# A trunk layer on one core: the fifth and sixth weight loads put behind splits on VectorE, and the last output bank finished in two halves

## The chip, the core and the metric

The kernel runs on one core of a Trainium2 chip. The core has TensorE for matrix products (PE; its weight loads are listed apart as PEld), VectorE (DVE), ScalarE (ACT), GpSimd (POOL) and SyncE (SP), which here issues nearly all transfers between HBM and on-chip memory; sixteen DMA engines carry them. Each engine works through its own list of instructions in order and waits on semaphores that the others raise. The metric is device microseconds of one execution.

## The reference

One decoder layer on 256 tokens of width 2048, in fp32: three groups of self-attention heads, cross-attention to a memory of 256 tokens, a gated feed-forward part with a short convolution, and a last RMS norm.

```python
h = rms_norm(x, g_mix)
qa, ka, va, qb, kb, vb, qc, kc, vc = split(h @ w_in)
x = x + concat(diff_attn(qa, ka, va), moba(qb, kb, vb), dilated(qc, kc, vc)) @ w_out
x = x + memory_cross_attention(rms_norm(x, g_cross), rms_norm(mem, g_mem), ...)
x = x + (silu(causal_dwconv3(h @ w_gate)) * (h @ w_up)) @ w_down     # h = rms_norm(x, g_ffn)
out = rms_norm(x, g_final)
```

## The kernel before

Every weight is streamed once from HBM. It is cut into **pieces** of 128 x 2048 fp32 (1 MB), numbered in the order in which they are used; piece 0 is the first, so the fifth and sixth are pieces 4 and 5. A piece lands in one of four buffers called `raw`. Before use it is split in two halves, h = 0 and 1: ACT copies half of `raw` to a rounded high part `hi` (L142), then DVE takes the difference as `lo` (L149). A product is then made of high times high, high times low and low times high. Half h of piece p has the number 2p + h, and **step i** of the main loop (L1023) multiplies half i: step 0 is the first half of piece 0, step 8 the first half of piece 4.

What is issued at a step, and so the order on each engine, is written out by hand: at step i the loop first asks for loads (L1027, L1028), then issues the split of half i + 4 (high parts on ACT, then what `before(i, ...)` registered, then low parts on DVE), then the products of half i, then what `after(i, ...)` registered.

At the start it is otherwise, since the inputs themselves come in: x (2 MB) and pieces 0, 1 and 2 are loaded in parts, taking turns (L933 to L946). For halves 2 to 7 the split is registered by `after(i, ...)` (L982), together with `put_x`, which scales two blocks of x into `hT` (L194 on ACT, L197 on DVE). Only from step 4 on does the main loop issue splits. So the split of half 8 (piece 4), which stands at the head of step 4, is on ACT's list **ahead** of the splits of halves 6 and 7 (piece 3), which stand behind the products of steps 4 and 5. On ACT this gives: half 5, half 8, x blocks, half 6, half 9, x blocks, half 7, a square of x, half 10 (piece 5), a square of x, half 11, and then four copies L354, with which the first chunk of output columns leaves PSUM.

The first chunk is done after step 7. It fills four PSUM banks; five are set aside for such chunks. Step 8 begins the second chunk: its first column block takes the free fifth bank, its second waits for the first bank of the old chunk, which is free after ACT's L354 and DVE's L355.

A fourth `raw` buffer is allocated at L950 as `hold`, and a copy of it at step 8 (L952) keeps it from the loads until then. So piece 3 goes into the buffer of piece 0, piece 4 into that of piece 1, piece 5 into that of piece 2, each when DVE has taken the last low part out of it.

At the end, `down` (L868) multiplies by w_down. All eight output banks (2 token tiles t, 4 column blocks n of 512) gather over 44 pieces; the products of the last two pieces are made bank by bank, and each bank is added to x as soon as it is whole (L890), squared (L891) and multiplied by the gain (L898). With all sums of a token tile in hand, three small DVE operations (L899 to L901) and a power on POOL (L903) give the factor r, and `finish` (L858) scales the four blocks and stores them.

Of the kernel before, what the change touches and what calls it, by code (L numbers as in the profile page):

```python
# [11 lines left out]
F32 = mybir.dt.float32  # L12
F32R = mybir.dt.float32r
AF = mybir.ActivationFunctionType
ALU = mybir.AluOpType
AX = mybir.AxisListType

P = 128
D = 2048
# [6 lines left out]
KF = DFF // P  # L26
# [8 lines left out]
HALF = 1024  # L35
NRAW = 4
# [26 lines left out]
def trunk(ctx, tc, x, mem, w_in, w_out, diff_lambda, rel_bias_table, w_cq, w_ckv, w_co, w_up, conv, w_down,  # L63
# [25 lines left out]
    def any_tile():  # L89

        turn[0] += 1
        return (acc_tile if turn[0] % 8 < NACC else at_tile)()

    def small(n, name, bufs=4):
        return tmp.tile([P, n], F32, tag=f"sm_{name}", name=name, bufs=bufs)
# [10 lines left out]
    pieces = []  # L106
# [6 lines left out]
    def new_raw(p):  # L113
        if p.raw is None:
            p.raw = wpool.tile([P, 2 * HALF], F32, tag="raw", name="raw", bufs=NRAW)

    def load(p):
        new_raw(p)
        at = 0
        for src in p.srcs:  # L120
            n = 1
            for _, c in src.ap[1:]:
                n *= c
            dst = p.raw[:, at:at + n]
            if len(src.ap) == 3:
                dst = dst.rearrange("p (k n) -> p k n", k=src.ap[1][1])
            SP.dma_start(dst, src)
            at += n
        assert at == 2 * HALF
# [28 lines left out]
    def before(i, f):  # L158
        pre.setdefault(i, []).append(f)

    def after(i, f):
        post.setdefault(i, []).append(f)
# [100 lines left out]
    def square_sum(src, acc, n=512):  # L263
        junk = tmp.tile([P, 512], mybir.dt.bfloat16, tag="junk", name="junk", bufs=1)
        ACT.activation(junk[:, :n], src, AF.Square, accum_out=acc)
# [557 lines left out]
    def xtok(t, c):  # L823

        return xT[:, 4 * c + 2 * t:4 * c + 2 * t + 2, :].rearrange("p k n -> p (k n)")
# [5 lines left out]
    outs = {}  # L831
# [11 lines left out]
        hi, lo = parts[k]  # L843
        DVE.tensor_tensor(lo, ffn["a"][:, k, :], hi.bitcast(F32), op=ALU.subtract)

    def down_mm(p, k, h, t, n):
        hi, lo = p.parts[h]
        ah, al = (a[:, t * P:(t + 1) * P] for a in parts[k])
        o = outs[t, 2 * h + n]
        wh, wl = hi[:, n * 512:(n + 1) * 512], lo[:, n * 512:(n + 1) * 512]  # L850
        PE.matmul(o, ah, wh, start=(k == 0), stop=False)  # L851
        PE.matmul(o, ah, wl, start=False, stop=False)  # L852
        PE.matmul(o, al, wh, start=False, stop=(k == KF - 1))  # L853

    ss3 = small(8, "ss3", 1)
    fin = {}

    def finish(n, t, og, r):  # L858
        col = slice(n * 512, (n + 1) * 512)
        if t and n % 2:  # L860
            DVE.scalar_tensor_tensor(og[:, col], xtok(t, n), r, gfin["t"][:, col], op0=ALU.mult, op1=ALU.mult)
        elif t or n < 2:
            ACT.activation(og[:, col], og[:, col], AF.Copy, scale=r)
        else:
            (DVE, POOL)[n - 2].tensor_scalar_mul(og[:, col], og[:, col], r)
        SP.dma_start(out[t * P:(t + 1) * P, col], og[:, col])

    def down(k):  # L868
        def f(p, h):
            if k == 0 and h == 0:  # L870
                for t in range(NT):
                    for n in range(4):
                        outs[t, n] = any_tile()
            fin[k] = p
            if k < KF - TAIL:
                for t in range(NT):
                    for n in range(2):
                        down_mm(p, k, h, t, n)
            elif k == KF - 1 and h == 1:
                done = None  # L880
                for t in range(NT):
                    og = wpool.tile([P, 2 * HALF], F32, tag="raw", name="raw", bufs=NRAW)
                    ms = small(2, "msf")
                    ss = ss3[:, 4 * t:4 * t + 4]
                    for n in range(4):
                        for kk in range(KF - TAIL, KF):
                            down_mm(fin[kk], kk, n // 2, t, n % 2)
                        col = slice(n * 512, (n + 1) * 512)
                        xc = xtok(t, n)
                        DVE.tensor_tensor(xc, outs[t, n], xc, op=ALU.add)  # L890
                        square_sum(xc, ss[:, n:n + 1])  # L891
                        if done:
                            for m in ((3, 0, 1), (2,), (), ())[n]:
                                finish(m, *done)
                        gains = ((), (0,), (), (2,)) if t else ((0,), (1,), (2,), (3,))
                        for m in gains[n]:
                            col = slice(m * 512, (m + 1) * 512)
                            DVE.tensor_tensor(og[:, col], xtok(t, m), gfin["t"][:, col], op=ALU.mult)  # L898
                    DVE.reduce_sum(ms[:, 0:1], ss[:, :3], axis=AX.X)  # L899
                    DVE.tensor_scalar(ms[:, 0:1], ms[:, 0:1], 1.0 / D, EPS, op0=ALU.mult, op1=ALU.add)  # L900
                    DVE.scalar_tensor_tensor(ms[:, 1:2], ss[:, 3:4], 1.0 / D, ms[:, 0:1], op0=ALU.mult, op1=ALU.add)  # L901
                    r = small(1, "rfin")
                    POOL.tensor_tensor(r, ms[:, 1:2], mhalf, op=ALU.pow)  # L903
                    done = t, og, r
                for n in range(4):
                    finish(n, *done)
        return f
# [38 lines left out]
    load_x(12, 4)  # L946

    hold = wpool.tile([P, 2 * HALF], F32, tag="raw", name="raw", bufs=NRAW)  # L950
    POOL.memset(hold[:, :1], 0.0)
    before(8, lambda: DVE.tensor_copy(small(1, "held", 1), hold[:, :1]))  # L952


    warm = acc_tile()
    for _ in range(24):
        PE.transpose(warm[:, :P], ident, ident)
# [3 lines left out]
    def put_x(k):  # L961
        for f in (high, low):
            for j in range(2):
                f(xblock(k + j), MIX, lambda: hT["h"], k + j)

    def split(i):
        split_hi(pieces[i // 2], i % 2)
        split_lo(pieces[i // 2], i % 2)
# [8 lines left out]
    put_x(2)  # L977
    split(1)
    load(pieces[3])
    nload = 4  # L980
    for i in range(6):
        after(i, lambda i=i: (put_x(2 * i + 4), split(i + 2)))  # L982
    for c in range(4):
        square_part(c + 5, "x", c, lambda c=c: xpart(c))
    norm_factors(10, "x")
# [37 lines left out]
    for i in range(2 * len(pieces)):  # L1023
        cur[0] = i
        new = []
        while nsplit < min(2 * len(pieces), i + 1 + LEAD if i > 2 else 0):
            while nload < len(pieces) and nload <= nsplit // 2 + NRAW - 2:  # L1027
                load(pieces[nload])  # L1028
                nload += 1
            new.append((pieces[nsplit // 2], nsplit % 2))  # L1030
            nsplit += 1
        for p, h in new:
            split_hi(p, h)
        for f in pre.pop(i, []):
            f()
        for p, h in new:
            split_lo(p, h)
        pieces[i // 2].mm(pieces[i // 2], i % 2)
        for f in post.pop(i, []):
            f()  # L1040
# [32 lines left out]
```

## Time and profile before

| what | value |
|---|---|
| time, median of three runs | 1251.67 us (1251.46 to 1252.79) |
| the profiled execution | 1252.27 us, of which the span is 1250.5 us |
| PE busy | 1235.8 us |
| DVE, ACT busy | 830.8 us, 630.0 us |
| the rest outside the span | 1.77 us |

A row of the timeline gives the start, the duration, the engine, the line, the operation and its tiles, and in brackets how long the engine sat idle before it and what ended that. "SPq" is SP issuing a transfer; the time until that transfer has landed stands in the row on DMA issues. TensorE's clock is given as the share of full speed that was granted: 1.00 is 2.4 GHz, 0.50 is 1.2 GHz.

### The profile page before, as it was taken

How to read it: one execution, taken by the hardware profiler on the slowest of the kernel's cores; microseconds unless marked ns; L12 is line 12 of the kernel's file. 1: busy time of each engine (PE TensorE's matmuls, PEld its weight loads, DVE VectorE, ACT ScalarE, POOL GpSimd, SP SyncE). 2: the span in 40 equal slices, each digit the busy share in tenths (PEclk: the TensorE clock that was granted, in tenths of full speed). 3: DMA queues.
4: the chain of work that ended last, by engine and by line, in shares of the span. 5: the costliest groups of instructions: out<-in, count | busy, mean ns of one | idle time of the engine just before them, and what ended most of it. 6: DMA issues, size and time to landing. Idle time of an engine off the chain costs nothing.

```text
span 1250.5 us, 17611 instructions
## 1 busy us (share of the span) xinstructions
PE 1235.8 (99%) x6928; PEld 1072.4 (86%) x6928; DVE 830.8 (66%) x1351; ACT 630.0 (50%) x979; POOL 12.3 (1%) x23
## 2 busy tenths in 40 slices
PE   8999999999999999999999999999999999999997
PEld 7888888988888899888888888888888888888885
DVE  5755676576568877876767768667776854445445
ACT  6544555556455656545445444444444544444444
POOL 0000000000000000000000000000000000000000
PEclk9999999999999999999999999999999999999998
DMA  7855554555566555565556565565556555555541
GB/s 275 273 172 191 189 170 159 182 184 156 177 227 217 170 169 164 204 206 169 170 201 196 175 202 190 183 201 184 187 180 202 192 193 180 200 176 194 187 150 68
DMA packets 104835, 233.26 MB, mean 187 GB/s; under 512 B 4208, under 2 KB 14768, under 8 KB 98992
## 3 DMA queue, kind: packets, MB, share of 16 engines
q1 hardware_dynamic: 104576, 231.85, 55.3%
q8 instruction: 54, 0.88, 0.3%
q10 hardware_dynamic: 144, 0.26, 0.1%
q14 instruction: 29, 0.24, 0.1%
q0 software_dynamic: 32, 0.02, 0.0%
HBM read 230.00 MB, written 2.12 MB: 186 GB/s over the span
## 4 chain that ended last, share of the span: by engine, by line
issue 58%; PE 37%; DMA 2%; DVE 2%; ACT 0%; POOL 0%; DVEq 0%; POOLq 0%; SPq 0%; ACTq 0%
PE acc L295 16%; PE acc L302 8%; PE acc L341 3%; PE acc L343 3%; PE acc L342 3%; DMA raw<-in_w_in 1%; PE at L401 1%; DMA xin<-in_x 1%; DVE lo L149 1%; PE at L420 0%; PE at L444 0%; DVE hT L197 0%; PE acc L298 0%; PE acc L297 0%; PE at L472 0%
## 5 line engine op out<-in xcount | busy, mean ns | idle before, releaser
L149 DVE TENSOR_TENSOR lo<-raw,hi 128x1024 fp32r<-128x1024 f32 x423 | 517.1, 1223 | 360.0 <-ACT hi L142 359.5
L142 ACT CAST hi<-raw 128x1024 fp32r<-128x1024 f32 x423 | 442.8, 1048 | 473.1 <-PE acc L295 272.4
L295 PE MATMUL acc<-hT,hi 128*128 128x512 f32 x1776 | 625.4, 395 | 3.5 <-ACT hi L142 3.3
L302 PE MATMUL acc<-hT,lo 128*128 128x256 f32 x1840 | 512.0, 280 | 0.6 <-DVE lo L149 0.6
L295 PEld LDWEIGHTS acc<-hT,hi 128*128 128x128 f32 x1776 | 334.4, 188 | 78.1 <-ACT hi L142 3.7
L302 PEld LDWEIGHTS acc<-hT,lo 128*128 128x128 f32 x1840 | 345.3, 188 | 1.4 <-DVE lo L149 1.2
L295 PE MATMUL at<-hT,hi 128*128 128x512 f32 x528 | 187.5, 392 | 0.0
L302 PE MATMUL at<-hT,lo 128*128 128x256 f32 x528 | 147.6, 280 | 0.0
L295 PEld LDWEIGHTS at<-hT,hi 128*128 128x128 f32 x528 | 99.1, 188 | 21.8
L302 PEld LDWEIGHTS at<-hT,lo 128*128 128x128 f32 x528 | 99.2, 188 | 0.0
L851 PE MATMUL acc<-hi,ah 128*128 128x512 f32 x220 | 87.8, 399 | 0.0
L853 PE MATMUL acc<-hi,al 128*128 128x512 f32 x220 | 86.7, 394 | 0.0
L852 PE MATMUL acc<-lo,ah 128*128 128x512 f32 x220 | 86.2, 392 | 0.0
L341 PE MATMUL acc<-hi,hT 128*128 128x256 f32 (+1 forms) x224 | 75.0, 335 | 0.0
L343 PE MATMUL acc<-hi,hT 128*128 128x256 f32 (+1 forms) x224 | 73.9, 330 | 0.0
L342 PE MATMUL acc<-lo,hT 128*128 128x256 f32 (+1 forms) x224 | 73.8, 330 | 0.0
L851 PE MATMUL at<-hi,ah 128*128 128x512 f32 x132 | 52.7, 399 | 0.0
L853 PE MATMUL at<-hi,al 128*128 128x512 f32 x132 | 52.0, 394 | 0.0
L788 ACT ACTIVATE y<-y 128x256 f32<-128x256 f32 x44 | 18.4, 419 | 66.3 <-DVE y L784 66.3
L852 PE MATMUL at<-lo,ah 128*128 128x512 f32 x132 | 51.7, 392 | 0.0
L853 PEld LDWEIGHTS acc<-hi,al 128*128 128x128 f32 x220 | 41.3, 188 | 10.8
L852 PEld LDWEIGHTS acc<-lo,ah 128*128 128x128 f32 x220 | 41.3, 188 | 9.8
(159 smaller groups left out, 1003.2 us busy)
## 6 DMA issues: line engine op xcount, KB each, us to landing
raw<-in_w_up SPq DMA_DIRECT2D x88, 1024.0 KB, 5.0
raw<-in_w_in SPq DMA_DIRECT2D x45, 1024.0 KB, 5.2
raw<-in_w_down SPq DMA_DIRECT2D x44, 1024.0 KB, 4.9
raw<-in_w_out SPq DMA_DIRECT2D x12, 1024.0 KB, 5.3
raw<-in_w_ckv SPq DMA_DIRECT2D x8, 1024.0 KB, 5.6
raw<-in_w_out SPq DMA_DIRECT2D x8, 512.0 KB, 4.9
raw<-in_w_cq SPq DMA_DIRECT2D x4, 1024.0 KB, 5.3
raw<-in_w_co SPq DMA_DIRECT2D x4, 1024.0 KB, 5.2
```

Of the source, the lines that this page charges most:

```text
L142: ACT.copy(hi, p.raw[:, h * HALF:(h + 1) * HALF])
L149: DVE.tensor_tensor(lo, p.raw[:, h * HALF:(h + 1) * HALF], hi.bitcast(F32), op=ALU.subtract)
L295: PE.matmul(accs[n], w, x, start=(i == 0), stop=False)
L302: PE.matmul(accs[n][:, :S], lo[:, j, n * P:(n + 1) * P], src()[:, korder[i], :S], start=False, stop=(i == len(korder) - 1))
L341: PE.matmul(o, xh, hi[:, j, :], start=(i == 0), stop=False)
L342: PE.matmul(o, xh, lo[:, j, :], start=False, stop=False)
L343: PE.matmul(o, xl, hi[:, j, :], start=False, stop=(i == len(korder) - 1))
L401: PE.matmul(out, a[u], b[w], start=first and i == 0, stop=last and i == 2)
L788: after(cur[0] + 1 + n, lambda: ACT.activation(gate[k], gate[k], AF.Silu))
L851: PE.matmul(o, ah, wh, start=(k == 0), stop=False)
L852: PE.matmul(o, ah, wl, start=False, stop=False)
L853: PE.matmul(o, al, wh, start=False, stop=(k == KF - 1))
```

## The change

At the start: `hold` and its copy at step 8 are gone, so that four `raw` buffers are in use from the beginning. Piece 3 is loaded into the free fourth buffer. Pieces 4 and 5 are no longer loaded by the main loop. A new function `load_behind` writes one column of the buffer by a DVE memset and then asks for the load; it is registered behind the split of half 5 (piece 4) and behind the split of half 7 (piece 5). The main loop asks for no load before step 6.

At the end: of the last bank (t = 1, n = 3) the products of the last two pieces are made for columns 0 to 255 first and then for columns 256 to 511, the latter in a bank of their own, and are added and squared apart. For t = 1 the gain products of blocks 2 and 3 stand behind the last additions, and the last scalings are done by ACT and DVE's simple multiply. For t = 0, ACT and POOL scale two blocks each.

```diff
-    def down_mm(p, k, h, t, n):
+    def down_mm(p, k, h, t, n, c0=0, c1=512, own=None):
...
-        PE.matmul(o, ah, wh, start=(k == 0), stop=False)
+        o, first = (outs[t, 2 * h + n][:, c0:c1], 0) if own is None else (own, KF - TAIL)
+        wh, wl = (a[:, n * 512 + c0:n * 512 + c1] for a in (hi, lo))
+        PE.matmul(o, ah, wh, start=(k == first), stop=False)
...
     def finish(n, t, og, r):
         col = slice(n * 512, (n + 1) * 512)
-        if t and n % 2:
-            DVE.scalar_tensor_tensor(og[:, col], xtok(t, n), r, gfin["t"][:, col], op0=ALU.mult, op1=ALU.mult)
-        elif t or n < 2:
+        if t:
+            if n % 2:
+                ACT.activation(og[:, col], og[:, col], AF.Copy, scale=r)
+            else:
+                DVE.tensor_scalar_mul(og[:, col], og[:, col], r)
+        elif n < 2:
             ACT.activation(og[:, col], og[:, col], AF.Copy, scale=r)
         else:
-            (DVE, POOL)[n - 2].tensor_scalar_mul(og[:, col], og[:, col], r)
+            POOL.tensor_scalar_mul(og[:, col], og[:, col], r)
         SP.dma_start(out[t * P:(t + 1) * P, col], og[:, col])
+
+    def gained(og, t, n):
+        col = slice(n * 512, (n + 1) * 512)
+        DVE.tensor_tensor(og[:, col], xtok(t, n), gfin["t"][:, col], op=ALU.mult)
...
+                    parts_of = ((0, 0, 512), (1, 0, 512), (2, 0, 512)) + (((3, 0, 256), (3, 256, 512)) if t else ((3, 0, 512),))
...
-    hold = wpool.tile([P, 2 * HALF], F32, tag="raw", name="raw", bufs=NRAW)
-    POOL.memset(hold[:, :1], 0.0)
-    before(8, lambda: DVE.tensor_copy(small(1, "held", 1), hold[:, :1]))
...
     load(pieces[3])
-    nload = 4
+    nload = 6
     for i in range(6):
         after(i, lambda i=i: (put_x(2 * i + 4), split(i + 2)))
+
+    def load_behind(p):
+        new_raw(p)
+        DVE.memset(p.raw[:, :1], 0.0)
+        load(p)
+
+    after(3, lambda: load_behind(pieces[4]))
+    after(5, lambda: load_behind(pieces[5]))
...
-            while nload < len(pieces) and nload <= nsplit // 2 + NRAW - 2:
+            while i > 5 and nload < len(pieces) and nload <= nsplit // 2 + NRAW - 2:
```

On SP the loads of pieces 3 to 7 stand in a row; the names in brackets are the semaphores that each load waits for (DMAHW a transfer, DVE and Activation those engines). Before:

```order
L924 DMA xin<-in_x 128x1024 [waits DMAHW4_49]
L127 DMA raw<-in_w_in 128x4x512 [waits DMAHW5_49,DVE_49]
L127 DMA raw<-in_w_in 128x4x512 [waits DMAHW6_49,DMAHW0_49,DVE_49]
L127 DMA raw<-in_w_in 128x4x512 [waits DMAHW3_49,DMAHW7_49,DMAHW2_49,DVE_49]
L127 DMA raw<-in_w_in 128x4x512 [waits DMAHW6_49,DVE_49]
```

On SP after the change, the same five places:

```order
L940 DMA xin<-in_x 128x1024 [waits DMAHW4_49]
L127 DMA raw<-in_w_in 128x4x512 [waits DMAHW5_49]
L127 DMA raw<-in_w_in 128x4x512 [waits DMAHW6_49,DVE_49,Activation_49]
L127 DMA raw<-in_w_in 128x4x512 [waits DMAHW0_49,DMAHW7_49,DVE_49,Activation_49]
L127 DMA raw<-in_w_in 128x4x512 [waits DMAHW3_49,DMAHW2_49,Activation_49]
```

The load of piece 3 no longer waits for DVE, those of pieces 4 and 5 still do, and the load of piece 6 stands behind that of piece 5.

What DVE is to have done by then is seen on its own list. DVE before, from the low part of half 5 to the copies that free the first banks (L149 is a low part, L197 a block of x, L227 a sum of squares, L355 such a copy):

```order
L149 TENSOR_TENSOR lo<-raw,hi 128x1024 x2
L197 SCALAR_TENSOR_TENSOR hT<-xin,hT 128x256 x2
L149 TENSOR_TENSOR lo<-raw,hi 128x1024 x2
L197 SCALAR_TENSOR_TENSOR hT<-xin,hT 128x256 x2
L149 TENSOR_TENSOR lo<-raw,hi 128x1024 x2
L227 TENSOR_TENSOR sq<-sq 128x1024
L149 TENSOR_TENSOR lo<-raw,hi 128x1024
L355 TENSOR_TENSOR mg<-acc,mg 128x256 x4
```

DVE after the change, the same stretch; the low parts are those of halves 5; 8; 6 and 9; 7; 10; 11:

```order
L149 TENSOR_TENSOR lo<-raw,hi 128x1024
L998 MEMSET raw 128x1
L149 TENSOR_TENSOR lo<-raw,hi 128x1024
L197 SCALAR_TENSOR_TENSOR hT<-xin,hT 128x256 x2
L149 TENSOR_TENSOR lo<-raw,hi 128x1024 x2
L197 SCALAR_TENSOR_TENSOR hT<-xin,hT 128x256 x2
L149 TENSOR_TENSOR lo<-raw,hi 128x1024
L998 MEMSET raw 128x1
L149 TENSOR_TENSOR lo<-raw,hi 128x1024
L227 TENSOR_TENSOR sq<-sq 128x1024
L149 TENSOR_TENSOR lo<-raw,hi 128x1024
L355 TENSOR_TENSOR mg<-acc,mg 128x256 x4
```

The first memset, with the load of piece 4 behind it, stands between the low parts of halves 5 and 8; the second memset, with the load of piece 5 behind it, now stands between the low parts of halves 7 and 10.

At the end, DVE's list for the second token tile, before (L890 adds a bank to x, L898 is a gain product, L861 a last scaling):

```order
L890 TENSOR_TENSOR xin<-acc,xin 128x512
L898 TENSOR_TENSOR raw<-xin,gfin 128x512
L899 TENSOR_REDUCE msf<-ss_92 128x1
L900 TENSOR_SCALAR msf<-msf 128x1
L901 SCALAR_TENSOR_TENSOR msf<-ss_92,msf 128x1
L861 SCALAR_TENSOR_TENSOR raw<-xin,rfin,gfin 128x512 x2
```

DVE at the end, after the change (L900 and L902 add to x, L873 is a gain product, L864 a last scaling):

```order
L900 TENSOR_TENSOR xin<-acc,xin 128x512
L902 TENSOR_TENSOR xin<-acc,xin 128x256
L910 TENSOR_REDUCE msf<-ss_92 128x1
L911 TENSOR_SCALAR msf<-msf 128x1
L873 TENSOR_TENSOR raw<-xin,gfin 128x512
L914 SCALAR_TENSOR_TENSOR msf<-ss_92,msf 128x1
L915 SCALAR_TENSOR_TENSOR msf<-ss_92,msf 128x1
L873 TENSOR_TENSOR raw<-xin,gfin 128x512
L864 TENSOR_SCALAR raw<-raw,rfin 128x512 x2
```

A gain product now stands between the small operations, another behind them, and the last scalings are of a simpler kind.

## Rows read from the trace of the kernel before

**Rows 1.** Page, costliest groups: count, busy us, mean ns, idle before and its releaser.

```profile
L149 DVE TENSOR_TENSOR lo<-raw,hi 128x1024 fp32r<-128x1024 f32 x423 | 517.1, 1223 | 360.0 <-ACT hi L142 359.5
L142 ACT CAST hi<-raw 128x1024 fp32r<-128x1024 f32 x423 | 442.8, 1048 | 473.1 <-PE acc L295 272.4
```

**Rows 2.** Waits of PE, whole span: us in total, times, longest us.

```profile
PE acc L295 <- ACT hi L142: 3.3, 1, 3.3
```

**Rows 3.** Chain that ended last, first 60 us: start us, us, what.

```profile
14.45 9.30 DMA raw<-in_w_in
23.85 1.05 ACT hi L142
...
28.14 0.58 PE acc L302
```

**Rows 4.** SP's issues of pieces 5, 6, 7; KB and us to landing below.

```profile
19.02 0.37 SPq L127 DMA_DIRECT2D raw<-in_w_in  x1
...
29.25 0.37 SPq L127 DMA_DIRECT2D raw<-in_w_in  x1
raw<-in_w_in SPq DMA_DIRECT2D x1, 1024.0 KB, 5.3
...
31.17 0.37 SPq L127 DMA_DIRECT2D raw<-in_w_in  x1
raw<-in_w_in SPq DMA_DIRECT2D x1, 1024.0 KB, 7.6
```

**Rows 5.** Timeline of ACT, high parts of halves 8 and 10.

```profile
23.85 1.05 ACT L142 CAST hi<-raw 128x1024 fp32r<-128x1024 f32 x1 [6.29 <-DMA raw<-in_w_in]
...
30.20 1.03 ACT L142 CAST hi<-raw 128x1024 fp32r<-128x1024 f32 x1
```

**Rows 6.** Timeline of DVE: low part of half 5, banks freed, copy of `hold`.

```profile
17.78 1.22 DVE L149 TENSOR_TENSOR lo<-raw,hi 128x1024 fp32r<-128x1024 f32 x1
...
35.02 1.50 DVE L355 TENSOR_TENSOR mg<-acc,mg 128x256 f32<-128x256 f32 x4
36.43 0.14 DVE L952 COPY held<-raw 128x1 f32<-128x1 f32 x1
```

**Rows 7.** Stretches of the start: length, busy us of each engine, granted clock (PEclk), DMA.

```profile
25.50:26.50 1.00, 0.00 (x0) 0.00 (x0) 1.00 (x3) 1.00 (x2) 0.00 (x0) 0.51 0.03 10
...
28.14:32.36 4.22, 4.22 (x14) 3.64 (x15) 4.11 (x5) 4.04 (x5) 0.00 (x0) 0.50 0.47 127
```

**Rows 8.** Timeline of PE: pairs of step 6 and of step 8.

```profile
30.43 0.63 PE L295 MATMUL acc<-hT,hi 128*128 128x512 f32 x1
...
31.07 0.63 PE L295 MATMUL acc<-hT,hi 128*128 128x512 f32 x1
...
35.83 0.39 PE L295 MATMUL acc<-hT,hi 128*128 128x512 f32 x1
...
36.18 0.39 PE L295 MATMUL acc<-hT,hi 128*128 128x512 f32 x1
```

**Rows 9.** Timeline of PE: products of 256 columns in a row; the last product.

```profile
108.05 0.28 PE L341 MATMUL acc<-hi,hT 128*128 128x256 f32 x1
108.17 0.28 PE L342 MATMUL acc<-lo,hT 128*128 128x256 f32 x1
...
1241.01 0.40 PE L853 MATMUL acc<-hi,al 128*128 128x512 f32 x1
```

**Rows 10.** Timeline of DVE and SP in the last 12 us.

```profile
1239.25 0.48 DVE L865 TENSOR_SCALAR raw<-raw,rfin 128x512 f32<-128x512 f32 x1
...
1242.06 0.68 DVE L898 TENSOR_TENSOR raw<-xin,gfin 128x512 f32<-128x512 f32 x1
...
1243.10 0.16 DVE L901 SCALAR_TENSOR_TENSOR msf<-ss,msf 128x1 f32<-128x1 f32 x1
...
1243.95 0.75 DVE L861 SCALAR_TENSOR_TENSOR raw<-xin,rfin,gfin 128x512 f32<-128x512 f32 x1 [0.69 <-POOL rfin L903]
...
1246.10 0.40 SPq L866 DMA_DIRECT2D out<-raw  x1
```

More of the change, by code (lines that the diff above doesn't have):

```diff
@@ L844, in a_low @@
         DVE.tensor_tensor(lo, ffn["a"][:, k, :], hi.bitcast(F32), op=ALU.subtract)
-    def down_mm(p, k, h, t, n):
+    def down_mm(p, k, h, t, n, c0=0, c1=512, own=None):
         hi, lo = p.parts[h]
         ah, al = (a[:, t * P:(t + 1) * P] for a in parts[k])
-        o = outs[t, 2 * h + n]
-        wh, wl = hi[:, n * 512:(n + 1) * 512], lo[:, n * 512:(n + 1) * 512]
-        PE.matmul(o, ah, wh, start=(k == 0), stop=False)
+        o, first = (outs[t, 2 * h + n][:, c0:c1], 0) if own is None else (own, KF - TAIL)
+        wh, wl = (a[:, n * 512 + c0:n * 512 + c1] for a in (hi, lo))
+        PE.matmul(o, ah, wh, start=(k == first), stop=False)
         PE.matmul(o, ah, wl, start=False, stop=False)
         PE.matmul(o, al, wh, start=False, stop=(k == KF - 1))
-    ss3 = small(8, "ss3", 1)
+    ss3 = small(10, "ss3", 1)
     fin = {}
@@ L883, in f @@
                     ms = small(2, "msf")
-                    ss = ss3[:, 4 * t:4 * t + 4]
-                    for n in range(4):
+                    ss = ss3[:, 5 * t:5 * t + 5]
+                    parts_of = ((0, 0, 512), (1, 0, 512), (2, 0, 512)) + (((3, 0, 256), (3, 256, 512)) if t else ((3, 0, 512),))
+                    for i, (n, c0, c1) in enumerate(parts_of):
+                        own = any_tile()[:, :c1 - c0] if c0 else None
                         for kk in range(KF - TAIL, KF):
[L887 to L891, printed above, removed]
+                            down_mm(fin[kk], kk, n // 2, t, n % 2, c0, c1, own)
+                        xc = xtok(t, n)[:, c0:c1]
+                        if own is None:
+                            DVE.tensor_tensor(xtok(t, n), outs[t, n], xtok(t, n), op=ALU.add)
+                        else:
+                            DVE.tensor_tensor(xc, own, xc, op=ALU.add)
+                        square_sum(xc, ss[:, i:i + 1], c1 - c0)
@@ L892, in f @@
                         if done:
-                            for m in ((3, 0, 1), (2,), (), ())[n]:
+                            for m in ((2, 0), (3, 1), (), (), ())[i]:
                                 finish(m, *done)
[L895 to L898, printed above, removed]
+                        if not t or n < 2:
+                            gained(og, t, n)
@@ L899, in f @@
                     DVE.reduce_sum(ms[:, 0:1], ss[:, :3], axis=AX.X)
                     DVE.tensor_scalar(ms[:, 0:1], ms[:, 0:1], 1.0 / D, EPS, op0=ALU.mult, op1=ALU.add)
-                    DVE.scalar_tensor_tensor(ms[:, 1:2], ss[:, 3:4], 1.0 / D, ms[:, 0:1], op0=ALU.mult, op1=ALU.add)
+                    if t:
+                        gained(og, t, 2)
+                        DVE.scalar_tensor_tensor(ms[:, 0:1], ss[:, 3:4], 1.0 / D, ms[:, 0:1], op0=ALU.mult, op1=ALU.add)
+                    DVE.scalar_tensor_tensor(ms[:, 1:2], ss[:, i:i + 1], 1.0 / D, ms[:, 0:1], op0=ALU.mult, op1=ALU.add)
@@ L902, in f @@
+                    if t:
+                        gained(og, t, 3)
                     r = small(1, "rfin")
```

## The prediction

> **What bounds the kernel now.** I read the waits of PE over the whole span first, then the chain of work that ended last, then the timelines of the first 60 and the last 15 us. Once it runs, PE waits for almost nothing: the only long wait in the middle of the program is one of 3.3 us for a high part from ACT [rows 2]. So whatever PE loses early is not made up later, since no slack stands behind it, and whatever it gains early is a gain at the end. The chain says where the 3.3 us come from: a load of a weight piece that takes 9.30 us from 14.45, then ACT's copy at 23.85, and PE goes on at 28.14 [rows 3]. The load issued at 14.45 is that of piece 4, not of piece 3. ACT had sat idle for 6.29 us before that copy [rows 5], because the high part of half 8 stands ahead of those of halves 6 and 7 on its list, and they could not pass it. Two things follow: at the start PE is held by the time at which piece 4 lands, and after it by piece 5, which ACT meets right behind half 7. A second loss rides on the first: the granted clock was 0.51 between 25.5 and 26.5 us, with PE empty, and still 0.50 in the 4.22 us from 28.14 on [rows 7].
>
> **The load of piece 4.** It now waits for a memset that DVE reaches only behind the low part of half 5. That one ran at 17.78 for 1.22 us [rows 6], to 19.0. It cannot come earlier: it follows splits of piece 2, whose load is ahead of piece 3's on SP and is not touched. The memset does not occur before; nearest to it is the copy of one column, 0.14 us [rows 6], so I take 0.1 us more after the overlap, and 0.05 to 0.2 as its bounds. The load is issued at 19.1 in place of 14.45. What it gains is that no other weights share the DMA engines with it. A load that was issued to empty engines at 29.25 took 5.3 us, one issued behind it at 31.17 took 7.6 [rows 4]. With 5.3 piece 4 lands at 24.4, against 14.45 + 9.30 = 23.75 before [rows 3], and ACT starts on it at 24.5, 0.65 us later than at 23.85 [rows 5]. The load of piece 3, issued some two microseconds earlier, is worth nothing: its copies stand behind half 8 on ACT.
>
> **The load of piece 5.** This is the large term. Its memset stands behind the low part of half 7. Before, that low part was what the load of piece 7 waited for (it went into piece 3's buffer), and this one was issued at 31.17 [rows 4]; so from ACT's start on half 8 at 23.85 [rows 5] to the end of that low part it is 7.3 us, all of it ACT and DVE working one after the other. Shifted by 0.65, it ends at 31.8, and the load of piece 5 is issued at 31.9 instead of 19.02 [rows 4]. With 5.3 us it lands at 37.2; ACT takes the high part of half 10 at 37.3 instead of 30.20 [rows 5], 7.1 us later. Behind that copy ACT holds the rest of the list: a square, the copy of half 11, and the four copies that empty the first chunk's banks.
>
> **How that reaches PE.** PE does not need piece 5 itself before step 10. It needs a bank. Step 8's first column block uses the free fifth one; the second waits for DVE's first L355, which before was at 35.02 [rows 6], over a microsecond ahead of PE's need at 36.18 [rows 8]. Now: 37.3, plus 1.05 for the copy of half 10, plus three operations on DVE (low part 10, the sum of squares, low part 11) of 1.22 each [rows 1], 3.5 together since each starts a little before the one ahead has ended, plus 0.4 for one of the four L355 in 1.50 us [rows 6]: 42.3. PE goes on 42.3 - 36.2 = 6.1 us later than before. The delay of 0.65 us at step 6 is contained in this and not added.
>
> **The clock after it.** PE will have been empty for some 5.5 us (from 36.18 + 0.65 = 36.8, when the first block is done, to 42.3), longer than the idle time that ended with a granted clock of 0.51 [rows 7]. So I expect a second stretch at the lower level. It costs what the first one did: at 0.50 a pair of products takes 31.07 - 30.43 = 0.64 us, at full clock 36.18 - 35.83 = 0.35 [rows 8]; in 4.22 us [rows 7] that is 6.6 pairs, each 0.29 us longer, 1.9 us. Bounds: 0, if the clock stays up, and 2.5, if it comes back a microsecond later. Start together: 6.1 + 1.9 = **8.0 us**.
>
> **The end.** The last bank's six products of 512 columns become twelve of 256. Such products ran 0.12 us apart [rows 9], twelve take 1.44 us, six of 512 about 1.40: PE ends at 1241.45 instead of 1241.41 (1241.01 + 0.40, [rows 9]). The first half's addition runs earlier on DVE, but it still takes all 512 columns, and DVE now has a second gain product ahead of it; the short addition then waits for that one's result, and a gain product of 0.68 us [rows 10] stands between the small operations. Counting these up from the last full addition, the last small operation falls at about 1243.2, against 1243.10 [rows 10]: no gain. What is gained is the last scaling on DVE, 0.48 instead of 0.75 us [rows 10], so that the first of four stores can go 0.27 us earlier; the other three follow it on SP as before, the last of them at 1246.10 [rows 10]. Net I take **-0.15 us**, bounds -0.5 and +0.5. The two scalings on POOL for t = 0 are hidden by PE's last products and by the square sums of t = 1; the removed `hold` copy (0.14 us) lay beside a PE that did not wait.
>
> **The sum.** +8.0 - 0.15 = +7.85 us. The profiled execution took 1252.27 us, of which 1250.5 are span; with the change 1260.1. It was 0.60 above the median of the three runs, so against the median 1251.67 it is **1259.5 us**, 0.63% slower. A difference under 0.2% (2.5 us) could not be told from none.
>
> **A rule that speaks for shorter loads.** In rows 4 a lone load of 1 MB takes 5.3 us. The Trainium skill, "DMA: Bandwidth & Descriptors", section "Anatomy of one DMA", fits loads issued from GpSimd as 2.0 us plus the bytes over 436 GB/s, which would make 4.4 us of 1 MB. By it, as an estimate, both waited-for loads would be 0.9 us shorter and the sum 1257.7. This trace, with loads issued from SP, does not agree: the row is 0.9 us longer, and I go by the row.
>
> **The rivals.**
> (a) *Piece 5 shares the engines.* The loads of pieces 6 and 7 follow that of piece 5 within a microsecond, as no buffer holds them back any more. If it then takes 7.6 us like the one at 31.17 [rows 4], 2.3 more: 1261.8. Against it: the load at 29.25, with another 1.9 us behind it, still took 5.3. Chance 0.17.
> (b) *The clock stays up* or falls late in the second gap: without the 1.9 us, 1257.6. Against it stand rows 7, after a shorter gap. Chance 0.17.
> (c) *Not slower: SP is not held by the memsets.* If the load were released by the buffer alone (piece 4's is piece 0's, free early; piece 5's is piece 1's, free at 14.45, [rows 3]), then pieces 3, 4 and 5 would follow one another without a gap, piece 4 would land up to 1 us before 23.75, piece 5 before ACT gets to it, and the time would be 1251.67 - 1.0 - 0.15 = 1250.5. It decides from the point where piece 5 lands before about 31, which with 5.3 us means an issue by 25.7. The order of SP shows DVE's semaphore on both loads, and the memset is the newest write to the buffer; so this would need an error of mine on what is waited for. Chance 0.06; a gain of over 2.5 us would need still more, 0.03 of it.
> (d) *The change does what it says and the wait goes:* piece 4, alone on the engines, lands well before 23.75. That needs a landing in under 4.6 us, which no row shows for 1 MB, and it leaves piece 5's wait in place, so that it would give about 1258. It is inside the range.
>
> **Chances.** The forecast (both gaps, second drop of the clock, 5.3 us) 0.60, (a) 0.17, (b) 0.17, (c) 0.06. The range takes in (a) and (b) with the bounds of the loads: low end 6.1 us, less 0.5 for loads of 5.0, less 0.5 at the end, no clock loss, 1251.67 + 5.1 = 1256.8; high end 6.1 + 2.3 + 2.5 - 0.15, 1262.4. Faster by over 0.2%: 0.03; within 0.2%: 0.04, from (c) and a little of the range's tail; slower: 0.93.
>
> **What would show it.** In the profile of the changed kernel: SP's load of piece 4 at about 19.1 and of piece 5 at about 31.9; ACT idle before the high part of half 8 until about 24.5 and again before that of half 10 until about 37.3; a second wait of PE, of about 5.5 us, on a product that starts a bank, put down to DVE's L355; a second stretch at half clock after 42; PE about 8 us later than before from 60 us to the end; the last store some 0.15 us nearer to PE's last product. Wrong if piece 5's load is issued before 26, if PE's second wait is under 3 us, or if the tail moves by over 0.5 us.

## The result, and the profile after

The changed kernel took 1260.87 us (median of 6 runs, 1259.59 to 1261.6), the kernel before 1252.01 in the same comparison (6 runs, 1251.39 to 1252.79): a ratio of 1.007, 95% interval 1.0057 to 1.0083, so 8.9 us slower. The prediction was 1259.5 with a range of 1256.8 to 1262.4. The profiled execution took 1260.19 us, 1258.4 of them span; the sum of the prediction, made against the profiled execution, was 1260.1.

Where the time came from is read in the same order as before. The waits of PE after the change, over the whole span (us in total, times, longest us):

```profile
PE acc L295 <- DVE mg L355: 5.3, 1, 5.3
PE acc L295 <- ACT hi L142: 3.5, 1, 3.5
```

The wait for ACT of [rows 2] is still there, 3.5 us instead of 3.3, and a second one of 5.3 us, for the first bank that DVE empties, has come. The chain that ended last, after the change (start us, us, what), shows what is behind them:

```profile
18.77 5.07 DMA raw<-in_w_in
...
23.94 1.05 ACT hi L142
...
31.23 0.04 DVE raw L998
...
31.34 5.29 DMA raw<-in_w_in
...
36.73 1.05 ACT hi L142
...
41.30 0.35 DVE mg L355
41.65 0.04 issue
41.70 0.80 PE acc L295
```

In the place of the one load of 9.30 us in [rows 3] stand two loads of 5.07 and 5.29 us, each behind a memset on DVE, and the second begins only when DVE is through with half 7. From there on it is one operation after the other: ACT's copy of half 10 at 36.73 instead of 30.20 [rows 5], the bank at 41.30 instead of 35.02 [rows 6], PE at 41.70 instead of 36.18 [rows 8].

PE around that gap, timeline after:

```profile
36.09 0.28 PE L302 MATMUL acc<-hT,lo 128*128 128x256 f32 x1
41.70 0.80 PE L295 MATMUL acc<-hT,hi 128*128 128x512 f32 x1 [5.32 <-DVE mg L355]
...
42.50 0.63 PE L295 MATMUL acc<-hT,hi 128*128 128x512 f32 x1
...
43.14 0.63 PE L295 MATMUL acc<-hT,hi 128*128 128x512 f32 x1
```

And the stretches there (length, busy us of PE, PEld, DVE, ACT and POOL, granted clock, DMA share, GB/s):

```profile
36.00:38.00 2.00, 0.37 (x3) 0.06 (x1) 0.19 (x1) 1.27 (x2) 0.00 (x0) 1.00 1.05 397
38.00:40.00 2.00, 0.00 (x0) 0.00 (x0) 2.00 (x2) 2.00 (x4) 0.00 (x0) 0.79 1.05 387
40.00:42.00 2.00, 0.30 (x1) 0.31 (x2) 2.00 (x5) 2.00 (x5) 0.00 (x0) 0.50 1.03 291
...
44.00:46.00 2.00, 2.00 (x7) 1.71 (x7) 2.00 (x2) 1.13 (x2) 0.00 (x0) 0.51 1.05 409
```

While PE is empty the granted clock falls to 0.50, the level of 1.2 GHz, and behind the gap a pair of products takes 0.64 us, as in the first half-speed stretch [rows 8], with the clock at 0.51 until 46.

The tail, DVE, POOL and ACT after the last product (which begins at 1248.79 and takes 0.28 us):

```profile
1250.82 0.16 DVE L915 SCALAR_TENSOR_TENSOR msf<-ss,msf 128x1 f32<-128x1 f32 x1
1250.90 0.68 DVE L873 TENSOR_TENSOR raw<-xin,gfin 128x512 f32<-128x512 f32 x1
1251.07 0.95 POOL L919 TENSOR_TENSOR rfin<-msf,mhalf 128x1 f32<-128x1 f32 x1 [1.33 <-DVE msf L915]
1252.05 0.88 DVE L864 TENSOR_SCALAR raw<-raw,rfin 128x512 f32<-128x512 f32 x2 [0.47 <-POOL rfin L919]
```

The same step before the change was this row of POOL's timeline:

```profile
1243.35 0.57 POOL L903 TENSOR_TENSOR rfin<-msf,mhalf 128x1 f32<-128x1 f32 x1 [3.15 <-DVE msf L901]
```

POOL's power took 0.95 us instead of 0.57, with the moved gain product beside it on DVE. From the end of the last product to the end of the span it is 1258.4 - 1249.07 = 9.33 us, before 1250.5 - 1241.41 = 9.09: the tail lost 0.24. What the start lost is read where PE begins the last bank, after the change and then before:

```profile
1247.47 0.28 PE L851 MATMUL acc<-hi,ah 128*128 128x256 f32 x1
```

```profile
1239.85 0.40 PE L851 MATMUL acc<-hi,ah 128*128 128x512 f32 x1
```

That is 7.62 us. Together 7.9, the difference of the spans.

### The profile page after: what moved, and what is told of

It is laid out like the page before. It is cut to its first block, busy times and chain, and to the rows that moved or that the text cites. A ratio compares the mean times of both kernels' runs of the same rounds, so it can differ in the third digit from the quotient of the medians.

```text
span 1258.4 us, 17634 instructions
## 1 busy us (share of the span) xinstructions
PE 1237.9 (98%) x6934; PEld 1074.3 (85%) x6934; DVE 831.8 (66%) x1355; ACT 630.8 (50%) x981; POOL 14.6 (1%) x23
## 4 chain that ended last, share of the span: by engine, by line
issue 58%; PE 37%; DVE 2%; DMA 2%; ACT 0%; POOL 0%; SPq 0%; POOLq 0%; ACTq 0%; DVEq 0%
PE acc L295 15%; PE acc L302 8%; PE acc L341 3%; PE acc L343 3%; PE acc L342 3%; DMA raw<-in_w_in 2%; DVE lo L149 1%; PE at L401 1%; DVE hT L197 1%; PE at L420 0%; PE at L444 0%; PE acc L297 0%; PE acc L298 0%; PE at L472 0%; ACT hi L142 0%
## 5 line engine op out<-in xcount | busy, mean ns | idle before, releaser
L149 DVE TENSOR_TENSOR lo<-raw,hi 128x1024 fp32r<-128x1024 f32 x423 | 517.4, 1224 | 367.4 <-ACT hi L142 367.0
L295 PE MATMUL acc<-hT,hi 128*128 128x512 f32 x1776 | 627.4, 396 | 9.1 <-DVE mg L355 5.3
L302 PE MATMUL acc<-hT,lo 128*128 128x256 f32 x1840 | 512.8, 281 | 0.6 <-DVE lo L149 0.6
L295 PEld LDWEIGHTS acc<-hT,hi 128*128 128x128 f32 x1776 | 335.2, 189 | 84.2 <-DVE mg L355 5.6
L302 PEld LDWEIGHTS acc<-hT,lo 128*128 128x128 f32 x1840 | 346.4, 189 | 1.4 <-DVE lo L149 1.2
L295 PE MATMUL at<-hT,hi 128*128 128x512 f32 x528 | 187.5, 392 | 0.0
L302 PE MATMUL at<-hT,lo 128*128 128x256 f32 x528 | 147.6, 280 | 0.0
L295 PEld LDWEIGHTS at<-hT,hi 128*128 128x128 f32 x528 | 99.0, 188 | 21.8
L302 PEld LDWEIGHTS at<-hT,lo 128*128 128x128 f32 x528 | 99.1, 188 | 0.0
L851 PE MATMUL acc<-hi,ah 128*128 128x512 f32 (+1 forms) x222 | 88.1, 397 | 0.0
L853 PE MATMUL acc<-hi,al 128*128 128x512 f32 (+1 forms) x222 | 87.0, 392 | 0.0
L852 PE MATMUL acc<-lo,ah 128*128 128x512 f32 (+1 forms) x222 | 86.6, 390 | 0.0
L851 PE MATMUL at<-hi,ah 128*128 128x512 f32 x132 | 52.7, 399 | 0.0
```

What stands on the lines that cost most here:

```text
L149: DVE.tensor_tensor(lo, p.raw[:, h * HALF:(h + 1) * HALF], hi.bitcast(F32), op=ALU.subtract)
L295: PE.matmul(accs[n], w, x, start=(i == 0), stop=False)
L302: PE.matmul(accs[n][:, :S], lo[:, j, n * P:(n + 1) * P], src()[:, korder[i], :S], start=False, stop=(i == len(korder) - 1))
L851: PE.matmul(o, ah, wh, start=(k == first), stop=False)
```

## The experiments

The theory: the late load of piece 5 makes the second wait, that gap costs a second fall of the clock, and the tail is next to nothing. Rivals: the late load of piece 4 is what costs; the tail is the loss; the clock behind the gap costs nothing.

### The two halves of the change apart

**e1_start**: the changed start with the old tail, the vector of partial square sums at its old 8 columns.

```diff
-    ss3 = small(10, "ss3", 1)
+    ss3 = small(8, "ss3", 1)
...  (finish, down_mm and down as before the change)
```

> The new start with the old end. My theory (the loss is made at the start, by the late load of piece 5): PE shows both waits, 3.5 us on a high part and 5.3 us on a freed bank, PE's last product comes 7.6 us later than before, and the time is 7.6 us above before, 1259.6; that is 0.25 us under the whole change. Rival (a good part of the loss is made at the end): 1258.5 or less.

Measured: 1268.41 us (before 1252.23), ratio 1.0127 (1.011 to 1.0144). That is slower than the whole change.

**e2_tail**: the old start with the changed tail.

```diff
+    hold = wpool.tile([P, 2 * HALF], F32, tag="raw", name="raw", bufs=NRAW)
+    POOL.memset(hold[:, :1], 0.0)
+    before(8, lambda: DVE.tensor_copy(small(1, "held", 1), hold[:, :1]))
...  (loads as before the change)
```

> The old start with the new end. My theory: from PE's last product to the end of the span 9.3 us instead of 9.1, so 0.25 us over before, 1252.3; not to be told from no change by the times, but by the trace: the power on POOL takes 0.95 us beside a gain product on VectorE instead of 0.57. As recorded: 0.15 us under before. Rival (the end costs or gains a microsecond): 1251.0 or 1253.0.

Measured: 1259.19 us, ratio 1.0054 (1.0039 to 1.0069). Both expectations failed, by 8.8 and 6.9 us, and the two halves together lose 23 us where the whole change loses 9. But the waits of PE were of the expected kind (in e1_start 3.5 us for ACT, as expected, and 4.5 for L355 instead of 5.3; in e2_tail none for L355). What had grown was PE's busy time: 1247.9 and 1241.7 us against 1235.8 before and 1237.9 after. Most products themselves had become slower, and not only at the start: between 700 and 900 us L302 on `acc` took 283 ns in e1_start against 280 before, and L295 397 ns in e2_tail against 392.

One thing differs there that is no part of the change's idea: the small vectors. `ss3` and the copy `held` together have 8 + 1 = 9 columns before, 10 in the changed kernel, 8 in e1_start and 10 + 1 = 11 in e2_tail, and what is allocated behind them should move by as much (this is read from the kernel; no trace shows an address). Three runs test that.

**e9_pad**: the kernel before, with two unused columns.

```diff
-    ss3 = small(8, "ss3", 1)
+    ss3 = small(10, "ss3", 1)
```

> The kernel before, instruction for instruction; only the vector of partial square sums is 10 floats wide instead of 8, two unused, so that what is placed behind it in SBUF lies where it lay in e2_tail. If addresses set the products' spacing: about 1258 to 1259, with L295 on acc near 400 ns and no new wait on TensorE. If they do not matter: 1252 (1251 to 1253).

Measured: 1259.09 us (1258.53 to 1260.94; before 1252.18), ratio 1.0051 (1.0035 to 1.0068), with no other line changed. The groups of PE by line, first the kernel before, then e9_pad (count, busy us and mean ns of one, idle before):

```profile
L295 PE MATMUL acc<-hT,hi 128*128 128x512 f32 x1776 | 625.4, 395 | 3.5 <-ACT hi L142 3.3 <-DVE hT L197 0.2
...
L851 PE MATMUL acc<-hi,ah 128*128 128x512 f32 x220 | 87.8, 399 | 0.0
```

```profile
L295 PE MATMUL acc<-hT,hi 128*128 128x512 f32 x1776 | 636.6, 400 | 5.1 <-ACT hi L142 4.4 <-DVE hT L197 0.7
...
L851 PE MATMUL acc<-hi,ah 128*128 128x512 f32 x220 | 85.4, 388 | 0.0
```

The products of L295 are 5 ns longer each, those of L851 11 ns shorter; there are eight times as many of the former, and L302 is longer too (282 ns instead of 280), so that PE is busy for 7.1 us more. (The profiled execution of e9_pad was the slowest of its four, 1260.94 us; the rest of what its span is longer by is mostly longer waits at the start.)

**e1b_start**: e1_start with the changed kernel's width, two columns unused.

```diff
-    ss3 = small(8, "ss3", 1)
+    ss3 = small(10, "ss3", 1)
```

> Again the change's start (fifth and sixth pieces loaded behind VectorE's splits of halves 5 and 7, no held buffer) with the final vector finished as before; the only difference from e1_start is that the vector of partial square sums is 10 floats wide as in the changed kernel, two of them unused, so that everything placed behind it in SBUF has the changed kernel's addresses. If the addresses cost e1_start its 9 us: products back to the same mean times as before (L295 on acc 395 ns, L302 280, L851 399), start +7.6, tail of before: 1259.6 (1258.5 to 1260.7). If the mixture of old tail and new start itself is slow (the rival): 1268 again, with L295 on acc at 398 ns.

Measured: 1259.8 us (1259.41 to 1260.28), ratio 1.0059 (1.0044 to 1.0074); L295 back at 395 ns.

**e2b_tail**: e2_tail with the copy in a column that exists already.

```diff
-    before(8, lambda: DVE.tensor_copy(small(1, "held", 1), hold[:, :1]))
+    before(8, lambda: DVE.tensor_copy(small(1, "first", 1), hold[:, :1]))
```

> Again before's start with the changed tail; the only difference from e2_tail is that the held copy goes into a scratch column that is already there, so that the small vectors fill 10 floats as in the changed kernel. If the addresses cost e2_tail its 7 us: 1252.3 (1251.3 to 1253.3), which is before plus the tail's 0.24; last product to end of span 9.3 (before 9.09), POOL's power 0.95 as in the changed kernel. If the mixture itself is slow: 1259 again, with L295 on acc at 400 ns.

Measured: 1252.75 us (1251.59 to 1253.38), ratio 1.0002 (0.9993 to 1.0011); L295 at 395 ns, last product to end of span 9.28. With the widths held still, the two halves are close to what the prediction made of them: the start costs 7.6 us, the tail next to nothing.

### Which load is it

**e3_p5**: the changed kernel, piece 5 loaded right behind piece 4, without a memset of its own.

```diff
-    after(5, lambda: load_behind(pieces[5]))
+    after(3, lambda: load(pieces[5]))
```

> The changed kernel, but piece 5 is loaded right behind piece 4, without a memset of its own. My theory: its load is issued near 19.2, lands near 27, ScalarE takes half 10 near 30.3 without idling, PE's second wait and the second drop of its clock are gone, and the time is 0.1 us (start) + 0.25 us (end) over before, 1252.4. Rival (the loss comes from four buffers, from the shared transfers behind piece 5 or from the first memset): it stays above 1256.

Measured: 1253.26 us (1252.23 to 1253.69), ratio 1.0007 (0.9997 to 1.0016). ACT takes half 10 in e3_p5 without having sat idle, at nearly the time of before (30.20, [rows 5]):

```profile
30.58 1.03 ACT L142 CAST hi<-raw 128x1024 fp32r<-128x1024 f32 x1
```

**e4_p4**: the changed kernel, piece 4 loaded as soon as its buffer is free.

```diff
-    after(3, lambda: load_behind(pieces[4]))
+    after(1, lambda: load(pieces[4]))
```

> The changed kernel, but piece 4 is loaded as soon as its buffer is free, without a memset; piece 5 stays behind its memset. My theory: piece 4 is issued near 10.4 and lands between 22.5 and 23.8; the first wait of PE shortens by 0.2 to 1.2 us, and since the load of piece 5 hangs on the same chain of splits, the whole moves by as much: 1259.6 to 1260.7, the second wait still 5.3 us. Rival (the first memset is the cause): 1253.

Measured: 1260.2 us (1259.85 to 1260.53), ratio 1.0062 (1.0047 to 1.0077). The waits of PE, first in e3_p5, then in e4_p4:

```profile
PE acc L295 <- ACT hi L142: 4.0, 1, 4.0
```

```profile
PE acc L295 <- DVE mg L355: 4.7, 1, 4.7
PE acc L295 <- ACT hi L142: 3.2, 1, 3.2
```

Taking the delay from piece 5 alone gives back 7.6 of the 8.9 us and takes the wait for L355 with it; taking it from piece 4 alone gives back nothing that can be told. The rival of piece 4 falls, and so do those of the four buffers and of the first memset, since e3_p5 keeps both.

The second wait in e4_p4 is 0.6 us shorter than expected, and PE goes on at 41.46 instead of 41.70, but this is lost again behind the gap. PE's timeline in e4_p4, where the pairs come back to their full pace:

```profile
46.75 0.58 PE L295 MATMUL acc<-hT,hi 128*128 128x512 f32 x1
...
47.29 0.40 PE L295 MATMUL acc<-hT,hi 128*128 128x512 f32 x1
```

Nine pairs took the 5.83 us from 41.46 to 47.29, which at 0.35 us apart would be 3.15; in the changed kernel it was seven pairs in the 4.48 us to 46.18, instead of 2.45. So the fall of the clock cost 2.7 us here and 2.0 there: its price was not the same in these two executions.

### Does the clock cost 1.9 us behind the gap

**e7_busy**: the changed kernel with 46 dummy transposes on TensorE in the second gap; nothing of the computation changes.

```diff
+NBUSY = 46
...
+                    if cur[0] == 8 and n == 1:
+                        idle = at_tile()
+                        for _ in range(NBUSY):
+                            PE.transpose(idle[:, :P], ident, ident)
```

> The changed kernel with 46 dummy transposes of 128x128 (about 0.11 us apart at full clock) put on TensorE ahead of step 8's second column block, in the 5.3 us in which it waits for the first L355; nothing else differs. If the second fall of the clock costs what the first one did (1.9 us): granted clock at 1.00 from 36 us on, first products behind the gap 0.35 us apart instead of 0.64, and 1258.9 (1258.2 to 1259.6), that is after's 1260.9 less 1.9. If the clock costs nothing there: 1260.8, as the changed kernel.

Measured: 1258.91 us (1258.46 to 1259.48), ratio to the kernel before 1.0056 (1.004 to 1.0071). PE's timeline in e7_busy:

```profile
35.96 5.18 PE L316 MATMUL at<-ident 128*128 128x128 f32 x46
41.48 0.50 PE L296 MATMUL acc<-hT,hi 128*128 128x512 f32 x1 [0.34 <-DVE mg L360]
...
41.93 0.39 PE L296 MATMUL acc<-hT,hi 128*128 128x512 f32 x1
...
42.28 0.39 PE L296 MATMUL acc<-hT,hi 128*128 128x512 f32 x1
```

And a stretch behind the gap (as above, with the granted clock third from the end):

```profile
42.00:44.00 2.00, 2.00 (x13) 1.75 (x13) 2.00 (x4) 0.86 (x2) 0.00 (x0) 1.00 0.81 285
```

The real work goes on at nearly the same time as in the changed kernel (41.48, there 41.70), but the granted clock is 1.00 throughout from 36 to 46 us, pairs run 0.35 us apart at once, and the span is 1256.2 instead of 1258.4. Of these 2.2 us 0.2 are the earlier start; the other 2.0 are what the fall of the clock behind the gap costs, beside the 5.3 us of waiting. By the medians the difference is 1260.87 - 1258.91 = 2.0.

### The tail

**e8b_tail**: e2b_tail with the last 512 columns scaled and multiplied by the gain in one DVE operation, so that no gain product runs beside POOL's power; ScalarE scales the second and third block.

```diff
-            if n % 2:
+            if n == 3:
+                DVE.scalar_tensor_tensor(og[:, col], xtok(t, n), r, gfin["t"][:, col], op0=ALU.mult, op1=ALU.mult)
+            elif n:
                 ACT.activation(og[:, col], og[:, col], AF.Copy, scale=r)
...
-                    if t:
-                        gained(og, t, 3)
```

> e2b_tail (before's start, the changed tail) without the gain product of the last 512 columns on VectorE: those columns are finished by VectorE in one operation with scale and gain, ScalarE scales the second and third quarter. POOL's power then runs with nothing beside it on VectorE. If the product beside it is what made the power 0.95 us: power back at 0.57, last product to end of span 8.9 instead of 9.28 (before 9.09). If POOL's power is slow for another reason (its own earlier work, its place): 0.95 again and 9.2 to 9.3.

POOL's power, first in e2b_tail, then in e8b_tail:

```profile
1243.42 0.95 POOL L919 TENSOR_TENSOR rfin<-msf,mhalf 128x1 f32<-128x1 f32 x1 [1.34 <-DVE msf L915]
```

```profile
1243.03 0.57 POOL L919 TENSOR_TENSOR rfin<-msf,mhalf 128x1 f32<-128x1 f32 x1 [1.34 <-DVE msf L917]
```

Without the product beside it the power is back at 0.57 us. POOL's own earlier work is no rival: its two scalings took 3.59 us in e2b_tail and 3.58 in e8b_tail. From the last product to the end of the span it is 1249.9 - 1241.04 = 8.86 us, 0.42 less than in e2b_tail and 0.23 less than before. (One run, 1251.7 us; a difference of this size is read from the trace, not from the time.)

### Can both waits go

**e5_order**: the kernel before, loads untouched; the splits of halves 8, 9 and 10 written behind those of halves 6 and 7.

```diff
-        while nsplit < min(2 * len(pieces), i + 1 + LEAD if i > 2 else 0):
+        while nsplit < min(2 * len(pieces), i + 1 + LEAD if i > 5 else 0):
```

> The kernel before, loads untouched; only the splits of halves 8, 9 and 10 are written behind those of halves 6 and 7 on ScalarE and VectorE, so that half 6 no longer stands behind the fifth piece's landing at 23.85. Theory (the wait of 4.7 us at step 6 is the order on ScalarE, not a lack of data; piece 3 is there at 21.1): that wait goes to under 1 us and with it the first clock drop (1.9 us): 1245.5 (1244.5 to 1247). Rival (the time is only moved: VectorE then reaches the first L355 later and TensorE waits there instead): 1250 to 1252, with a wait for L355 of 3 us or more.

Measured: 1249.53 us (1247.67 to 1249.83), ratio 0.9974 (0.9963 to 0.9986). The median lies above the expected range. In the profiled execution (1247.67 us) the first wait and the first fall of the clock are gone as expected (granted 1.00 from 20 to 46 us), and the rival is there in part: PE waits for the first L355, which DVE reaches only behind four low parts and a sum of squares. The wait of PE in e5_order, then DVE's timeline:

```profile
PE acc L295 <- DVE mg L355: 1.4, 1, 1.4
```

```profile
25.30 3.50 DVE L149 TENSOR_TENSOR lo<-raw,hi 128x1024 fp32r<-128x1024 f32 x3 [0.50 <-ACT hi L142]
28.71 1.22 DVE L227 TENSOR_TENSOR sq<-sq 128x1024 f32<-128x1024 f32 x1
29.84 1.22 DVE L149 TENSOR_TENSOR lo<-raw,hi 128x1024 fp32r<-128x1024 f32 x1
30.98 1.42 DVE L355 TENSOR_TENSOR mg<-acc,mg 128x256 f32<-128x256 f32 x4
```

4.1 us of waits gone, 1.4 new, 1.8 less busy time of PE: 4.5 of the 4.6 us by which the span is shorter. The expectation had left out the 1.4 and counted 4.7 us of waiting at step 6, where the waits add up to 4.1 (PE makes one product in between, at 26.70). Four of the six runs lie at 1249.5 to 1249.8, two at 1247.7 and 1248.1; what the slower four did, no trace shows, and it stays open.

**e10_lead**: as e5_order, with fewer splits ahead of the first L354 and L355.

```diff
-        while nsplit < min(2 * len(pieces), i + 1 + LEAD if i > 2 else 0):
+        while nsplit < min(2 * len(pieces), i + 1 + LEAD - {6: 2, 7: 2, 8: 1}.get(i, 0) if i > 5 else 0):
```

> As e5_order, on the kernel before, but with fewer splits ahead of the first bank's L354 and L355: at step 6 only half 8, at step 7 half 9, at step 8 halves 10 and 11, from step 9 on as before. In e5_order TensorE still waited 1.4 us for the first L355 (30.98), which stood behind the splits of halves 10 and 11. Theory (every one of these waits is the order of the splits on ScalarE and VectorE): that wait falls to 0.4 us or less and nothing new comes, 1.0 to 1.4 us under e5_order's 1249.5: 1248.3 (1247.3 to 1249). Rival (half 10 now comes too late for step 10): a wait for ACT hi or DVE lo after 34 us of more than 1 us, and 1249.5 or more.

Measured: 1247.37 us (1247.06 to 1247.47; before 1252.16), ratio 0.9961 (0.9949 to 0.9974). The wait for L355 is gone; besides one of 1.4 us at the very start, which the kernel before has too, PE waits only here:

```profile
PE at L241 <- DVE sq L236: 1.0, 1, 1.0
```

**e11_lead**: the changed kernel with the same one line.

```diff
-        while nsplit < min(2 * len(pieces), i + 1 + LEAD if i > 2 else 0):
+        while nsplit < min(2 * len(pieces), i + 1 + LEAD - {6: 2, 7: 2, 8: 1}.get(i, 0) if i > 5 else 0):
```

> The changed kernel, its late loads and memsets and its tail untouched, with the split order of e10_lead. The fifth piece should still be issued near 18.8 and land near 23.9, the sixth be issued behind the split of half 7, now near 24.9, and land near 30.3. Theory (the late loads cost nothing by themselves; they cost because half 8 stands ahead of halves 6 and 7, and half 10 ahead of the first L354, on ScalarE): neither wait is left (each under 0.5 us), no clock drop, and the time is e10_lead's plus the tail's 0.2 to 0.3: 1248.6 (1247.5 to 1250). Rival (a load behind a split is late whatever the order): a wait for ACT hi of 3 us or more stays, 1255 or more.

Measured: 1247.52 us (1247.36 to 1247.7), ratio 0.9963 (0.9951 to 0.9976). The wait of PE that is left in e11_lead, and the timelines of DVE and then of ACT there:

```profile
PE at L241 <- DVE sq L236: 1.1, 1, 1.1
```

```profile
24.53 0.06 DVE L998 MEMSET raw<- 128x1 f32 x1
...
29.19 1.41 DVE L355 TENSOR_TENSOR mg<-acc,mg 128x256 f32<-128x256 f32 x4
```

```profile
27.55 0.36 ACT L354 COPY mg<-acc 128x256 f32<-128x256 f32 x1
...
30.77 1.99 ACT L142 CAST hi<-raw 128x1024 fp32r<-128x1024 f32 x2
```

The changed loads are all still there: piece 4 is issued at 19.35 and takes 5.2 us, piece 5 at 24.68 and takes 5.4. But half 8 no longer stands ahead of halves 6 and 7, so DVE's memset for piece 5 comes at 24.53 instead of 31.18, and the copy of half 10 stands behind L354 and not ahead of it, so the bank does not wait for piece 5. Piece 5 lands at 30.1, and ACT takes half 10 at 30.77 without having waited. The same stretch, first after the change, then in e11_lead:

```profile
20.00:28.00 8.00, 4.06 (x21) 2.91 (x19) 2.99 (x4) 4.06 (x7) 0.00 (x0) 0.84 0.36 129
...
40.00:46.00 6.00, 4.30 (x13) 3.73 (x14) 6.00 (x9) 3.98 (x7) 0.00 (x0) 0.50 0.97 322
```

```profile
20.00:28.00 8.00, 8.00 (x49) 7.04 (x48) 5.42 (x8) 6.98 (x9) 0.00 (x0) 1.00 0.68 205
...
40.00:46.00 6.00, 6.00 (x37) 5.34 (x37) 2.43 (x4) 1.94 (x2) 1.61 (x1) 1.00 1.05 386
```

In both stretches PE is busy throughout, at full clock. Both kernels, with one line changed, are faster than the kernel before, by 4.8 and 4.6 us, and they cannot be told from one another: in this order the late loads cost nothing that can be told. What is left is new and small: 1.0 to 1.1 us in which PE waits for a sum of squares (L236) that now comes late on DVE. The expectation of no new wait failed there; e10_lead came 0.9 us under its expected time all the same, since its base, e5_order, had four of its six runs near 1249.7.

## Why the prediction was right, step by step

- **The load of piece 4.** Predicted issued at 19.1 and landing at 24.4; it was issued at 18.77 and landed at 23.84. DVE came to the low part of half 5 at 17.44 instead of 17.78 [rows 6], which the prediction had held impossible; in e11_lead, with the same loads up to there, it came at 18.03, so that this is the spread of single executions. The load took 5.07 us instead of 5.3. ACT began half 8 at 23.94, practically as before (23.85, [rows 5]); the term of 0.65 was too large by 0.56, and with it everything behind.
- **The load of piece 5.** 7.3 us from ACT's start on half 8 to the end of the low part of half 7 were predicted; from 23.94 to 31.23 it was 7.29. 5.3 us of load were predicted, it was 5.29. Rival (a), sharing with the loads behind it, did not come: those of pieces 6 and 7 were issued at 31.81 and 32.36, and took 7.5 and 9.9 us themselves. The estimate of 4.4 us for 1 MB, by the fit for loads issued from GpSimd in the Trainium skill, "DMA: Bandwidth & Descriptors", section "Anatomy of one DMA", did not come here either, with loads issued from SP; the loads that PE waited on took 5.07 and 5.29, in e11_lead 5.2 and 5.4. Rival (c) did not come: the loads were issued at 18.77 and 31.34, each right behind its memset (18.61 and 31.18), and e3_p5 shows that without the second memset the load of piece 5 comes early and the wait is gone.
- **The way to PE.** 5.0 us from ACT's start on half 10 to the end of the first L355 were predicted (37.3 to 42.3), 4.92 measured (36.73 to 41.65). PE went on at 41.70 instead of 36.18, 5.5 us later, against 6.1: the 0.6 from piece 4.
- **The clock.** 1.9 us predicted; 7.62 - 5.52 = 2.1 by the trace of after, 2.0 by e7_busy. Rival (b), that the clock stays up, did not come. The size was in part luck: in e4_p4 the same fall cost 2.7, over the prediction's upper bound of 2.5.
- **The start together**: 8.0 predicted, 7.62 measured.
- **The tail**: -0.15 predicted, +0.24 measured. The last small operation came 1.75 us after the last product, before 1.69: no gain, as worked out. From the last scaling's start to the first of the four stores it was 0.52 us instead of 0.75: the gain of 0.27 was nearly there. The step that failed is what was not on the list at all: POOL's power was taken as it was, and beside the gain product it took 0.38 us more. The bound of +0.5 held it.

The errors of start (0.38 too much) and tail (0.39 too little) cancel in the sum by luck, which is why the profiled execution was met to 0.1 us; by the medians the change costs 1 us more than the sum, which is the spread of single runs around them (the profiled run after was 0.7 under its median, that of before 0.3 over).

The prediction's sentence that the earlier load of piece 3 "is worth nothing", as its copies stand behind half 8 on ACT, was the one that led on: e5_order, e10_lead and e11_lead are that sentence turned round.

## What to carry to other kernels

Before a load is tied to a point in an engine's list, read what stands ahead of that point and what the engine that uses the data will hold back when it comes late: here PE did not need piece 5 for another two steps, but the copies that free its banks stood behind it. On engines that work in order, a late transfer can be cured by the place of its consumer as well as by its own: here the load moved forward gave 1253.26 us (e3_p5), the splits moved back 1247.52 (e11_lead), since this took the first wait away too. And when two kernels differ in what they allocate, compare the mean time of the same products first: a version that undoes half of a change must keep the layout of the other half, or it measures the layout.

## What the runs showed that was not expected

**Two unused columns change the pace of products.** Two unused fp32 columns in a small vector (e9_pad) made the same instructions 6.9 us slower (0.5%) on medians; L295 went from 395 to 400 ns, L851 from 399 to 388. In the runs with 9 and 10 such columns (all but three) the mean of L295 on the `acc` banks is 394 to 396 ns, with 8 (e1_start) 398 and with 11 (e2_tail, e9_pad) 400. That addresses are the cause is argued, not shown: the width is all that e9_pad changes, but no trace shows an address. Which address would matter, that of weights, inputs or both, was not tried.

**POOL beside VectorE.** The power on one column took 0.57 us with VectorE idle and 0.95 us when a gain product of 512 columns (0.68 us, two inputs in SBUF) ran on VectorE, in after and in e2b_tail alike. Not every operation of VectorE does this. The power for the other token tile ran beside an addition of the same size whose one input is a PSUM bank, and took 0.55 us (after the change):

```profile
1245.33 0.69 DVE L900 TENSOR_TENSOR xin<-at,xin 128x512 f32<-128x512 f32 x1
...
1245.49 0.55 POOL L919 TENSOR_TENSOR rfin<-msf,mhalf 128x1 f32<-128x1 f32 x1 [722.99 <-DVE msf L915]
```

The slow power began beside the gain product, and ended 0.44 us after it (1250.90 + 0.68 = 1251.58, power's end 1252.02). The Trainium skill, "SBUF — State Buffer", section "SBUF: two separate sides", says that a VectorE operation with two SBUF inputs and a GpSimd operation that reads SBUF take turns on a shared pair of ports, the later one being blocked for the whole instruction. These rows agree: begun after the product, the power ended a little after it, and e8b_tail, without the product, has the 0.57 back.
